# Two layers of gated DeltaNet, short convolution and SwiGLU on one core: other PSUM banks for the side products of two heads, a scaling on another engine, and weight casts in another place

## The chip, the cores and the metric

The kernel runs on one core of one Trainium2 chip. The time is the device time of one execution in microseconds (us); the number that counts is the median of several executions. All arithmetic is in float32. The products of the projections and of the FFN are made of three matmuls each: an operand is cut into a rounded part `hi` and a remainder `lo`, and `hi*hi`, `hi*lo` and `lo*hi` are added in PSUM.

## The reference, cut to what matters

x has 1024 positions of 1024 columns; there are two layers. Each layer is

```
h = rms_norm(x); proj = h @ w_in
q, k, v  = silu(causal conv of 4 taps)            # 4 heads of 128 columns each
o_dn     = gated delta rule of q, k, v, g, beta   # a recurrence over the positions, by chunks
o_sc     = gate_b * conv3(gate_c * hv), normed    # 4 groups of 128 columns
x = x + concat(o_dn normed * silu(z), o_sc) @ w_out
x = x + (silu(rms_norm(x) @ w_gate) * (rms_norm(x) @ w_up)) @ w_down
```

and one last rms_norm follows. The gated delta rule keeps a 128x128 state S per head: S_t = a_t S_{t-1} (I - b_t k_t k_t^T) + b_t v_t k_t^T, o_t = S_t q_t. Each chunk needs the products K K^T and Q K^T of its keys and queries with the decay on them, and keys and values with the positions on the partitions.

## The kernel before, in words

**Halves and chunks.** The 1024 positions are two halves of 512, and a half is four chunks of 128. A tile is mostly 128x512: 128 columns of a head on the partitions and the 512 positions of a half.

**The mixer.** `head(hd, group)` runs the projections of k, q and v for both halves of a head (`kvq`, line 488; 24 matmuls of 128x512 each, two PSUM banks tagged `mm` in turn), each followed by the convolution and the silu on ScalarE (ACT) and VectorE (DVE). The side products of a head are jobs that are put in between the matmuls: after every projection matmul `tick` counts the jobs' lags down, and a job whose lag has run out issues its next piece behind the matmul last issued. They are, for each half:

- `key_tok` (513): four PE transposes of k into one bank, tagged `aux`; ACT copies it out as `kdec` (519) and takes four sums of squares (502).
- `query_tok` (522): four transposes of q into `fx`, and four sums of squares on ACT.
- `gram` (570): K K^T into `aux` (tile `gk`) and Q K^T into `fx` (tile `gq`), each four matmuls of 128x128; DVE multiplies each with the decay into `U` and `A` (584). At its end DVE makes the factor `kd` (587) and scales all of `kdec` with it (588).
- `value_tok` (591): four transposes of v into `aux`, and one DVE operation that reads them (597).

`aux` and `fx` are one bank each (line 75: PS), so that a side product can't be written before the one ahead of it in the same bank has been read. Heads 0 and 1 come first; then `group(0)` inverts and merges (aux) and runs the recurrence `chain` (669) over both, in the banks `ch0`, `ch1` (the steps) and `o0`, `o1` (the outputs). Heads 2 and 3 are projected meanwhile, with their side products in aux and fx. While heads 0 and 1 make their side products, no chain runs: ch0, ch1, o0 and o1 are free, but for the transposes of x's second half at the start of layer 0 (`x_half1`, 319). The short convolution (`sconv`, `sc_norm`) and `gate` use fx and aux too, and `ba` (372) uses fx.

**The FFN's down.** Products are formed by a scheme of seven products P1 to P7 in place of eight (Winograd's form of Strassen's), with the hidden state's operands spilled to HBM and read back (`bprep`, 1145). Twelve blocks (loop of 1210) of seven products handle 18 of the 22 rows of tiles; the last four rows, `tail` (1193), are multiplied plainly at the end (tile `pd`, 1283 to 1288), for each half and each of eight output tiles: four pairs of operand and weight, three matmuls a pair. For these, `tail_half(half)` (1196) loads the hidden operands (`ft`), casts `hi_f` on ACT (897) and subtracts `lo_f` on DVE (898). Half 0's operands are made in the last blocks (1224, 1229); half 1's by `tail_half(1)` at line 1278. Behind it lines 1279 and 1280 load the four weight tiles (`raw_d`, 512 KB each, a ring of three buffers), cast `hi_d` on ACT (195) and subtract `lo_d` on DVE (196). The first `pd` matmuls go into an `mm` bank, which the products P4 and P3 of the last block have just used and which DVE reads at line 1237 (`xT`).

**Order.** Each engine has one queue that it works off strictly in order, the DMA issues among them on SP. The order of every queue is fixed when the kernel is built: a scheduler goes through its own timing of the program and gives each engine, whenever it is free, the instruction that stands first in the program among those that are ready there (operands made, buffer free). So a line's place in the program is its priority, not its place in the queue. `with tc.issue_after(ins)` also puts the instructions that are written in its block and run on the engine of `ins` behind `ins` in that queue, and leaves the other engines' alone.

Of the kernel before, what the change touches and what calls it, by code (L numbers as in the profile page):

```python
# [11 lines left out]
AF = mybir.ActivationFunctionType  # L12
ALU = mybir.AluOpType
# [4 lines left out]
P = 128  # L18
# [33 lines left out]
def tile_hybrid(ctx, tc, x, norm1_g, w_in, dn_conv_w, dn_a_log, dn_dt_bias, dn_norm_g,  # L52
# [3 lines left out]
    V, S, G, PE = nc.vector, nc.scalar, nc.gpsimd, nc.tensor  # L56
# [20 lines left out]
    def sb(tag, name, shape=(P, HALF), dt=F32):  # L77
        if tag == "h":
            return hpool.tile([P, HALF], dt, tag=tag, name=name)
        if tag == "pre":  # L80

            t = prep_.tile([P, 16 + HALF], dt, tag=tag, name=name)
            return t[0:shape[0], 0:shape[-1]] if len(shape) == 2 else t[:, 0:HALF].rearrange("p (c i) -> p c i", i=shape[-1])
        if tag in PB:
            return phase[0].tile(list(shape), dt, tag=tag, bufs=PB[tag], name=name)
        return wp.tile(list(shape), dt, tag=tag, bufs=SB[tag], name=name)
# [5 lines left out]
    def ps_(tag, name, shape=(P, HALF)):  # L92
        return pp.tile(list(shape), F32, tag=tag, bufs=PS[tag], name=name)
# [52 lines left out]
    def full_ap(t):  # L146
        return dram_ap(t, 0, [[128, 128], [USZ, 4], [1, 128]])
# [25 lines left out]
    def split_w(view, name, kd=KD, w=P, eng=None, tags=None):  # L173

        raw = ring.tile([P, kd, w], F32, tag="raw", bufs=3, name=f"raw_{name}")
        dma(raw, view)
        return split_raw(raw, name, eng, tags)
# [12 lines left out]
    def split_raw(raw, name, eng=None, tags=None):  # L190
        if tags:
            hi, lo = [sb(t, f"{p}_{name}", list(raw.shape), F32R) for t, p in zip(tags, ("hi", "lo"))]
        else:
            hi, lo = w_pair(list(raw.shape), name)
        S.copy(hi, raw)
        (eng or V).tensor_tensor(lo, raw, hi.bitcast(F32), ALU.subtract)
        return hi, lo
# [15 lines left out]
    def row_r(ssq, name, stream="n"):  # L213

        m = sm.tile([P, 4], F32, tag="rr", bufs=2, name=f"rr_{name}")
        V.tensor_scalar(m, ssq, 1.0 / D, EPS, ALU.mult, ALU.add)
        y = sm.tile([P, 4], F32, tag="rowr", bufs=4, name=f"rowr_{name}")
        V.tensor_copy(y, rsqrt(m, [P, 4], name, stream))
        return y
# [128 lines left out]
    for l in range(DEPTH):  # L348

        with tc.tile_pool(name=f"mixer{l}", bufs=1, side="right") as phase[0]:  # L350
            w_l = w_in[l]
            hs = [h0, h1]
            sh4 = [P, 4, P]
# [4 lines left out]
            def fx(name, shape=(P, HALF)):  # L358
                return ps_("fx", name, shape)

            def bank(tag):
                return lambda name, shape: ps_(tag, name, shape)

            def wcols(c0, n=P):
                return w_l[:, c0:c0 + n].rearrange("(k p) c -> p k c", p=P)
# [119 lines left out]
            units = {}  # L485
# [12 lines left out]
            def sumsq(ps, dst, nm):  # L498

                sq = sb("sqp", f"sq{nm}", sh4)  # L500
                for c in range(4):
                    S.activation(sq[:, c, :], ps[:, c, :], AF.Square, accum_out=dst[:, c:c + 1])

            def transposed(src, nm, bank):
                t = bank(nm, sh4)
                for c in range(4):
                    PE.transpose(t[:, c, :], src[:, c * P:(c + 1) * P], ident)
                return t
# [4 lines left out]
            def key_tok(hd, half):  # L513

                nm = f"{l}_{hd}_{half}"
                u, ss = units[hd, half], stat(hd)["ss"]
                ktok = transposed(u["k"], f"ktok_{nm}", aux)
                u["kdec"] = sb("kdec", f"kdec_{nm}", sh4)
                S.copy(u["kdec"], ktok)
                sumsq(ktok, ss[:, half * 4:half * 4 + 4], f"k_{nm}")  # L520

            def query_tok(hd, half):
                nm = f"{l}_{hd}_{half}"
                qtok = transposed(units[hd, half]["q"], f"qtok_{nm}", fx)
                sumsq(qtok, stat(hd)["ss"][:, 8 + half * 4:12 + half * 4], f"q_{nm}")

            stats_of = {}
# [1 line left out]
            def stat(hd):  # L529
                if hd not in stats_of:  # L530
                    nm = f"{l}_{hd}"
                    stats_of[hd] = {"ss": s8("ss", nm, 2, 16), "gl": s8("gl", nm, 3)}
                return stats_of[hd]
# [36 lines left out]
            def gram(hd, half, slot):  # L570

                nm = f"{l}_{hd}_{half}"
                u = units[hd, half]
                h4 = slice(half * 4, half * 4 + 4)
                row, c2 = u["row"], u["c2"][:, h4]
                V.tensor_tensor(row, row, c2.unsqueeze(2).broadcast_to(sh4), ALU.mult)
                U = sb("U", f"U_{nm}", sh4)
                A = sb("A", f"A_{nm}", sh4)
                for src, dst in (("k", U), ("q", A)):
                    gp = ps_({"k": "aux", "q": "fx"}[src], f"g{src}_{nm}", sh4)  # L580
                    for c in range(4):
                        cs = slice(c * P, (c + 1) * P)
                        PE.matmul(gp[:, c, :], lhsT=u["k"][:, cs], rhs=u[src][:, cs], start=True, stop=True)
                    V.tensor_tensor(dst, gp, row, ALU.mult)
                dma(full_ap(ud[slot]), U)
                G.tensor_tensor(u["q"], u["q"], u["eta"].rearrange("p c i -> p (c i)"), ALU.mult)
                V.tensor_tensor(u["kd"], u["kd"], c2, ALU.mult)
                V.tensor_tensor(u["kdec"], u["kdec"], u["kd"].unsqueeze(2).broadcast_to(sh4), ALU.mult)
                u.update(U=U, A=A)

            def value_tok(hd, half):
                nm = f"{l}_{hd}_{half}"
                u = units[hd, half]
                h4 = slice(half * 4, half * 4 + 4)
                vtok = transposed(u["v"], f"vtok_{nm}", aux)
                v2 = sb("v2", f"v2_{nm}", sh4)
                V.scalar_tensor_tensor(v2, vtok, 0.5, u["irk"][:, h4].unsqueeze(2).broadcast_to(sh4),
                                       ALU.mult, ALU.mult)
                u["v2"] = v2
# [265 lines left out]
        with tc.tile_pool(name=f"ffn{l}", bufs=1, side="right") as phase[0]:  # L865
# [18 lines left out]
            def stats(acc, name):  # L884
# [3 lines left out]
                        PE.matmul(sp[:, c:c + 1], lhsT=acc[i][:, c * P:(c + 1) * P], rhs=ones1, start=i == 0, stop=i == 1)  # L888
                return row_r(sp[:, 0:4], name)

            def split(src, tags, name, eng=V):
                res = []
                for tag, p in zip(tags, ("hi", "lo")):
                    nm = f"{p}_{name}"
                    res.append(hpool.tile([P, HALF], F32R, tag="h", name=nm) if tag == "h"
                               else sb(tag, nm, (P, HALF), F32R))
                S.copy(res[0], src)  # L897
                eng.tensor_tensor(res[1], src, res[0].bitcast(F32), ALU.subtract)  # L898
                return res

# [124 lines left out]
            for half in range(2):  # L1025
                nm = f"{l}_{half}"
# [22 lines left out]
            for half in range(2):  # L1049
                nm = f"{l}_{half}"  # L1050
# [31 lines left out]
                if half == 0:  # L1082
                    for k in (0, 2, 4, 6, 1, 3, 5, 7):
                        scaled(k)
                        q = "P2" if k % 2 else "P1"
                        B[q].append(split(xh[k], BT[q][k // 2], f"h{q}_{l}_{k}", G))
                else:
# [5 lines left out]
                    def opnd(q, j, src):  # L1093
                        B[q].append(split(src, BT[q][j], f"h{q}_{l}_{j}"))
# [44 lines left out]
            def staged(src, name):  # L1139
                t = sb(STG[stage_n[0] % len(STG)], name)  # L1140
                stage_n[0] += 1
                dma(t, src[:])
                return t

            def bprep(g, q, ops):
                ops[q] = []
                for j in range(GJ):
                    t = staged(hsd[g * GJ + j][q], f"st{q}_{l}_{g}_{j}")
                    ops[q].append(split(t, BT2[q][j], f"d{q}_{l}_{g}_{j}"))
# [43 lines left out]
            tail = list(range(NG * GJ * 2, NF))  # L1193
            hid = {}

            def tail_half(half, part=slice(None)):
                for m in tail[part]:
                    t = staged(hsd[m // 2][("P1", "P2", "P4", "P3")[half * 2 + m % 2]], f"ft{l}_{half}_{m}")
                    hid[half, m] = split(t, (("k", "q"), ("kdec", "v2"))[m % 2] if half else ("h", "h"), f"f{l}_{half}_{m}")
# [10 lines left out]
            for g in range(NG):  # L1210
                for dp in range(4):
                    n = g * 4 + dp
                    nm = f"d{l}_{g}_{dp}"
# [33 lines left out]
            def end(half, acc):  # L1247
# [15 lines left out]
                for c in range(4):  # L1263
# [3 lines left out]
                    for kk in range(2):  # L1267
# [6 lines left out]
                        else:  # L1274
                            V.tensor_scalar(xo, pf, r[:, c:c + 1], None, ALU.mult)
                    dma(out[0, ts_, :], xt)

            tail_half(1)
            wdn = [split_w(ffn_w_down[l][m * P:(m + 1) * P, :].rearrange("p (k c) -> p k c", c=P), f"d{l}_{m}",
                           tags=None if m > tail[0] else ("ub", "yb")) for m in tail]  # L1280
            acc = [[sb("pre", f"acc1_{l}_{h}")] for h in range(2)]
            xg = [[], []]
            for half in range(2):
# [41 lines left out]
```

## Time and profile before

| | us |
|---|---|
| median of 3 runs | 2419.73 |
| lowest, highest run | 2418.4, 2421.8 |
| the profiled execution: its own time | 2423.16 |
| the profiled execution: its span, from first to last instruction | 2421.5 |
| mean granted TensorE clock, as a share of full speed | 0.987 |

The profile is of one execution, which took 3.43 us more than the median; 1.66 us of its time lie outside its span. In its rows a group or an instruction stands as engine, line of the kernel, operation, output<-inputs and shape; a bracket at the end is the idle time of that engine before it and what ended it. A row of the waits gives who waited (engine, tile, line), for what, the total in us, the number of times and the longest. PEclk is the TensorE clock that was granted, as a share of full speed; it has two levels, 1.2 and 2.4 GHz, and a stretch between 0.5 and 1 had some of both. In a timeline, "x4" are four instructions merged.

### The profile page before, as it was taken

The numbers are of one execution on the slowest core, as the hardware profiler recorded it, in microseconds if no ns is written. First come the engines' busy times: TensorE is split into PE (matmuls) and PEld (weight loads), VectorE is DVE, ScalarE is ACT, GpSimd is POOL, SyncE is SP. The second block draws the span as 40 slices with busy tenths as digits, with TensorE's granted clock in tenths as the row PEclk, the third lists the DMA queues.
The fourth block names the chain that finished last, engine by engine and source line by source line (L and its number), as shares of the span: only waits on it lengthen the run. The fifth ranks groups of instructions, "written<-read, shape, count | busy, mean of one in ns | idle before, by whom it ended". The sixth has DMA issues, their size and how long they took to land.

```text
span 2421.5 us, 31888 instructions
## 1 busy us (share of the span) xinstructions
PE 2340.7 (97%) x11522; PEld 1908.2 (79%) x11522; DVE 1622.2 (67%) x2870; ACT 910.3 (38%) x1917; POOL 602.3 (25%) x492
## 2 busy tenths in 40 slices
PE   7999999999999999999998999999999999999998
PEld 5787787887788888788777778878878888887877
DVE  7775773767655655799776666646685565568994
ACT  5524523534323223443344244234342322334334
POOL 3000000031444433234221001000325443422350
PEclk8999999999999999999999999999999999999999
DMA  7222223652333323744322312338423332346531
GB/s 228 66 65 71 65 63 90 204 183 61 109 118 105 113 87 98 248 144 146 106 69 71 76 49 69 77 92 251 124 75 119 106 113 87 109 137 220 160 101 70
DMA packets 362167, 275.21 MB, mean 114 GB/s; under 512 B 47343, under 2 KB 295449, under 8 KB 362009
## 3 DMA queue, kind: packets, MB, share of 16 engines
q1 hardware_dynamic: 362008, 273.18, 37.4%
q8 instruction: 90, 1.47, 0.3%
q14 instruction: 69, 0.56, 0.1%
HBM read 198.08 MB, written 75.04 MB: 113 GB/s over the span
## 4 chain that ended last, share of the span: by engine, by line
PE 73%; DVE 12%; issue 6%; DMA 4%; POOL 3%; ACT 2%; SPq 0%; DVEq 0%; POOLq 0%; ACTq 0%
PE P_g L205 16%; PE P_u L205 14%; PE P_d L205 7%; PE po L205 5%; PE ps_csc L205 4%; PE ps_bsc L205 4%; PE ps_hsc L205 4%; PE pd L205 3%; PE ps_v L205 3%; PE ps_z L205 2%; PE ps_k L205 2%; PE ps_q L205 2%; DMA stP<-hs_P 2%; DMA row<-gd 2%; DVE xT L1237 1%
## 5 line engine op out<-in xcount | busy, mean ns | idle before, releaser
L205 PE MATMUL P_g<-hi_hP,hi_P_g 128*128 128x512 f32 x608 | 239.5, 394 | 3.4 <-DVE u_g L995 1.9
L205 PE MATMUL P_g<-lo_hP,hi_P_g 128*128 128x512 f32 x608 | 238.7, 393 | 3.6 <-DVE lo_hP L898 3.6
L205 PE MATMUL P_u<-hi_hP,hi_P_u 128*128 128x512 f32 x608 | 237.6, 391 | 3.1 <-DVE c_g L1011 2.2
L205 PE MATMUL P_u<-lo_hP,hi_P_u 128*128 128x512 f32 x608 | 237.3, 390 | 0.0
L205 PE MATMUL P_u<-hi_hP,lo_P_u 128*128 128x512 f32 x608 | 237.1, 390 | 0.0
L205 PE MATMUL P_g<-hi_hP,lo_P_g 128*128 128x512 f32 x608 | 236.4, 391 | 0.0
L205 PE MATMUL P_d<-hi_dP,lo_P_d 128*128 128x512 f32 x504 | 196.8, 390 | 3.3 <-DVE lo_P_d L928 3.3
L205 PE MATMUL P_d<-hi_dP,hi_P_d 128*128 128x512 f32 x504 | 196.7, 390 | 2.2 <-ACT hi_dP L897 1.5
L205 PE MATMUL P_d<-lo_dP,hi_P_d 128*128 128x512 f32 x504 | 196.6, 390 | 0.9 <-DVE lo_dP L898 0.9
L205 PEld LDWEIGHTS P_g<-hi_hP,hi_P_g 128*128 128x128 f32 x608 | 114.9, 189 | 30.6 <-DVE u_g L995 2.8
L205 PEld LDWEIGHTS P_g<-lo_hP,hi_P_g 128*128 128x128 f32 x608 | 115.0, 189 | 28.7 <-DVE lo_hP L898 5.2
L205 PEld LDWEIGHTS P_u<-hi_hP,hi_P_u 128*128 128x128 f32 x608 | 114.6, 189 | 28.5 <-DVE c_g L1011 3.1
L205 PEld LDWEIGHTS P_g<-hi_hP,lo_P_g 128*128 128x128 f32 x608 | 114.9, 189 | 23.7
L205 PEld LDWEIGHTS P_u<-lo_hP,hi_P_u 128*128 128x128 f32 x608 | 114.7, 189 | 23.9
L205 PEld LDWEIGHTS P_u<-hi_hP,lo_P_u 128*128 128x128 f32 x608 | 114.4, 188 | 23.7
L1237 DVE TENSOR_TENSOR xT<-P_d,xT 128x512 f32<-128x512 f32 x192 | 125.1, 678 | 3.1 <-PE P_d L205 3.1
L927 ACT CAST hi_P_g<-m_g 128x1024 fp32r<-128x1024 f32 (+1 forms) x64 | 58.8, 919 | 151.9 <-PE P_u L205 127.7
L205 PEld LDWEIGHTS P_d<-hi_dP,lo_P_d 128*128 128x128 f32 x504 | 94.6, 188 | 25.0 <-DVE lo_P_d L928 5.8
L205 PEld LDWEIGHTS P_d<-hi_dP,hi_P_d 128*128 128x128 f32 x504 | 94.6, 188 | 23.6 <-ACT hi_dP L897 2.8
L205 PEld LDWEIGHTS P_d<-lo_dP,hi_P_d 128*128 128x128 f32 x504 | 94.6, 188 | 21.8 <-DVE lo_dP L898 2.2
L898 DVE TENSOR_TENSOR lo_dP<-stP,hi_dP 128x512 fp32r<-128x512 f32 x126 | 96.6, 790 | 18.0 <-ACT hi_dP L897 17.8
L897 ACT CAST hi_dP<-stP 128x512 fp32r<-128x512 f32 x126 | 75.2, 620 | 74.4 <-DMA stP<-hs_P 71.0
(410 smaller groups left out, 5872.0 us busy)
## 6 DMA issues: line engine op xcount, KB each, us to landing
stP<-hs_P SPq DMA_DIRECT2D x126, 256.0 KB, 3.8
m_g<-in_ffn_w_gate_dram SPq DMA_DIRECT2D x46, 512.0 KB, 4.1
m_u<-in_ffn_w_up_dram SPq DMA_DIRECT2D x44, 512.0 KB, 4.4
hs_P<-t SPq DMA_DIRECT2D x72, 256.0 KB, 2.4
m_d<-in_ffn_w_down_dram SPq DMA_DIRECT2D x48, 384.0 KB, 4.1
hs_P<-c_u SPq DMA_DIRECT2D x70, 256.0 KB, 2.0
raw_o<-in_w_out_dram SPq DMA_DIRECT2D x32, 512.0 KB, 4.8
xd<-xT SPq DMA_DIRECT2D x32, 256.0 KB, 2.3
```

The lines of the kernel that those rows point to most:

```text
L205: last_mm[0] = PE.matmul(ps, lhsT=w(k)[i], rhs=m(k)[j], start=k + i + j == 0, stop=k + i == n).ins
L897: S.copy(res[0], src)
L898: eng.tensor_tensor(res[1], src, res[0].bitcast(F32), ALU.subtract)
L927: S.copy(hi, src)
L1237: V.tensor_tensor(t, ps, t, ALU.add)
```

## The change

The side products of heads 0 and 1 (`hd < 2`) go to the recurrence's banks: k's transposes to ch0, q's to ch1, K K^T to o0 and Q K^T to o1. The transposes of v stay in aux for half 0, and go to fx for half 1. Heads 2 and 3 keep aux and fx. For all heads the scaling of kdec becomes four ACT activations of 128x128, one for each chunk, with the factor as a scale per partition. The loads, casts and subtractions of down's last four weights are written ahead of `tail_half(1)`, with their ACT casts behind the last `hi` cast of an operand written before them.

```diff
@@ -358,8 +358,9 @@
             def fx(name, shape=(P, HALF)):
                 return ps_("fx", name, shape)
 
-            def bank(tag):
-                return lambda name, shape: ps_(tag, name, shape)
+            def side(hd, free, tag):
+
+                return lambda name, shape: ps_(free if hd < 2 else tag, name, shape)
 
             def wcols(c0, n=P):
                 return w_l[:, c0:c0 + n].rearrange("(k p) c -> p k c", p=P)
@@ -514,14 +515,14 @@
 
                 nm = f"{l}_{hd}_{half}"
                 u, ss = units[hd, half], stat(hd)["ss"]
-                ktok = transposed(u["k"], f"ktok_{nm}", aux)
+                ktok = transposed(u["k"], f"ktok_{nm}", side(hd, "ch0", "aux"))
                 u["kdec"] = sb("kdec", f"kdec_{nm}", sh4)
                 S.copy(u["kdec"], ktok)
                 sumsq(ktok, ss[:, half * 4:half * 4 + 4], f"k_{nm}")
 
             def query_tok(hd, half):
                 nm = f"{l}_{hd}_{half}"
-                qtok = transposed(units[hd, half]["q"], f"qtok_{nm}", fx)
+                qtok = transposed(units[hd, half]["q"], f"qtok_{nm}", side(hd, "ch1", "fx"))
                 sumsq(qtok, stat(hd)["ss"][:, 8 + half * 4:12 + half * 4], f"q_{nm}")
 
             stats_of = {}
@@ -577,7 +578,7 @@
                 U = sb("U", f"U_{nm}", sh4)
                 A = sb("A", f"A_{nm}", sh4)
                 for src, dst in (("k", U), ("q", A)):
-                    gp = ps_({"k": "aux", "q": "fx"}[src], f"g{src}_{nm}", sh4)
+                    gp = {"k": side(hd, "o0", "aux"), "q": side(hd, "o1", "fx")}[src](f"g{src}_{nm}", sh4)
                     for c in range(4):
                         cs = slice(c * P, (c + 1) * P)
                         PE.matmul(gp[:, c, :], lhsT=u["k"][:, cs], rhs=u[src][:, cs], start=True, stop=True)
@@ -585,14 +586,15 @@
                 dma(full_ap(ud[slot]), U)
                 G.tensor_tensor(u["q"], u["q"], u["eta"].rearrange("p c i -> p (c i)"), ALU.mult)
                 V.tensor_tensor(u["kd"], u["kd"], c2, ALU.mult)
-                V.tensor_tensor(u["kdec"], u["kdec"], u["kd"].unsqueeze(2).broadcast_to(sh4), ALU.mult)
+                for c in range(4):
+                    S.activation(u["kdec"][:, c, :], u["kdec"][:, c, :], AF.Copy, scale=u["kd"][:, c:c + 1])
                 u.update(U=U, A=A)
 
             def value_tok(hd, half):
                 nm = f"{l}_{hd}_{half}"
                 u = units[hd, half]
                 h4 = slice(half * 4, half * 4 + 4)
-                vtok = transposed(u["v"], f"vtok_{nm}", aux)
+                vtok = transposed(u["v"], f"vtok_{nm}", (fx if hd < 2 and half else aux))
                 v2 = sb("v2", f"v2_{nm}", sh4)
                 V.scalar_tensor_tensor(v2, vtok, 0.5, u["irk"][:, h4].unsqueeze(2).broadcast_to(sh4),
                                        ALU.mult, ALU.mult)
@@ -888,13 +890,15 @@
                         PE.matmul(sp[:, c:c + 1], lhsT=acc[i][:, c * P:(c + 1) * P], rhs=ones1, start=i == 0, stop=i == 1)
                 return row_r(sp[:, 0:4], name)
 
+            last_hi = [None]
+
             def split(src, tags, name, eng=V):
                 res = []
                 for tag, p in zip(tags, ("hi", "lo")):
                     nm = f"{p}_{name}"
                     res.append(hpool.tile([P, HALF], F32R, tag="h", name=nm) if tag == "h"
                                else sb(tag, nm, (P, HALF), F32R))
-                S.copy(res[0], src)
+                last_hi[0] = S.copy(res[0], src).ins
                 eng.tensor_tensor(res[1], src, res[0].bitcast(F32), ALU.subtract)
                 return res
 
@@ -1275,9 +1279,10 @@
                             V.tensor_scalar(xo, pf, r[:, c:c + 1], None, ALU.mult)
                     dma(out[0, ts_, :], xt)
 
+            with tc.issue_after(last_hi[0]):
+                wdn = [split_w(ffn_w_down[l][m * P:(m + 1) * P, :].rearrange("p (k c) -> p k c", c=P), f"d{l}_{m}",
+                               tags=None if m > tail[0] else ("ub", "yb")) for m in tail]
             tail_half(1)
-            wdn = [split_w(ffn_w_down[l][m * P:(m + 1) * P, :].rearrange("p (k c) -> p k c", c=P), f"d{l}_{m}",
-                           tags=None if m > tail[0] else ("ub", "yb")) for m in tail]
             acc = [[sb("pre", f"acc1_{l}_{h}")] for h in range(2)]
             xg = [[], []]
             for half in range(2):
```

## Rows read from the trace of the kernel before

**Rows 1.** The page, part 1: busy time and share of the span, by engine.

```profile
PE 2340.7 (97%) x11522; PEld 1908.2 (79%) x11522; DVE 1622.2 (67%) x2870; ACT 910.3 (38%) x1917; POOL 602.3 (25%) x492
```

**Rows 2.** The waits of the PE queue: us in total, times, longest.

```profile
PE ktok L507 <- DVE U L584: 7.5, 2, 3.8
...
PE pd L205 <- DVE lo_d L196: 4.7, 2, 2.3
...
PE pd L205 <- DVE xT L1237: 3.6, 2, 1.8
...
PE vtok L507 <- DVE v L597: 2.3, 3, 1.0
...
PE ot L507 <- ACT sqk L502: 2.1, 2, 1.1
...
PE yp L648 <- ACT R L642: 1.8, 2, 0.9
...
PE vtok L507 <- DVE U L584: 1.5, 1, 1.5
```

**Rows 3.** The timeline of PE, side products of heads 0 and 1: start, us, what.

```profile
100.89 1.11 PE L507 MATMUL ktok<-ident,kT_k 128*128 128x128 f32 x4 [3.84 <-DVE U L584]
...
1286.70 0.66 PE L507 MATMUL ktok<-ident,kT_k 128*128 128x128 f32 x4 [3.70 <-DVE U L584]
...
1288.12 1.07 PE L583 MATMUL gq<-qT_q,kT_k 128*128 128x128 f32 x8
```

**Rows 4.** The timeline of DVE in layer 1, around the U product.

```profile
1282.53 1.28 DVE L588 TENSOR_TENSOR kdec<-kdec,kd 128x512 f32<-128x512 f32 x2
1283.73 1.65 DVE L196 TENSOR_TENSOR lo_z<-raw_z,hi_z 128x1024 fp32r<-128x1024 f32 x1
...
1285.97 0.68 DVE L584 TENSOR_TENSOR U<-gk,row 128x512 f32<-128x512 f32 x1
...
1287.30 0.68 DVE L584 TENSOR_TENSOR A<-gq,row 128x512 f32<-128x512 f32 x1
```

**Rows 5.** Busy time by stretch, PE PEld DVE ACT POOL, PEclk, DMA; stretches of 10 us.

```profile
100.00:110.00 10.00, 9.12 (x46) 7.93 (x47) 7.12 (x16) 5.18 (x18) 1.97 (x3) 0.83 0.56 143
1280.00:1290.00 10.00, 6.30 (x40) 5.15 (x38) 9.84 (x16) 5.95 (x17) 3.04 (x3) 1.00 0.37 92
```

**Rows 6.** Line 588 on DVE: ns min/median/max.

```profile
L588 DVE TENSOR_TENSOR kdec<-kdec,kd x16: 674/684/692, 96.7 to 1497.4; 128x512 f32<-128x512 f32 x16
```

**Rows 7.** The timeline of ACT: four 128x128 activations on SBUF, layer 0.

```profile
84.21 1.26 ACT L567 ACTIVATE row<-row,ngl 128x128 f32<-128x128 f32 x4
```

**Rows 8.** The timeline of PE at the end of down, layer 0.

```profile
1166.12 0.50 PE L205 MATMUL pd<-hi_f,hi_d 128*128 128x512 f32 x1 [1.77 <-DVE xT L1237]
...
1171.24 0.50 PE L205 MATMUL pd<-hi_f,lo_d 128*128 128x512 f32 x1 [2.33 <-DVE lo_d L196]
```

**Rows 9.** The timeline of DVE at the end of down, layer 0.

```profile
1164.80 0.67 DVE L898 TENSOR_TENSOR lo_f<-ft,hi_f 128x512 fp32r<-128x512 f32 x1
1165.40 0.67 DVE L1237 TENSOR_TENSOR xT<-P_d,xT 128x512 f32<-128x512 f32 x1
1166.00 3.46 DVE L898 TENSOR_TENSOR lo_f<-ft,hi_f 128x512 fp32r<-128x512 f32 x3
...
1169.98 1.21 DVE L196 TENSOR_TENSOR lo_d<-raw_d,hi_d 128x1024 fp32r<-128x1024 f32 x1
```

**Rows 10.** The timeline of ACT at the end of down, layer 0.

```profile
1150.62 1.05 ACT L195 CAST hi_d<-raw_d 128x1024 fp32r<-128x1024 f32 x1 [3.51 <-POOL m_d L959]
...
1152.73 0.62 ACT L897 CAST hi_f<-ft 128x512 fp32r<-128x512 f32 x1
...
1162.36 1.05 ACT L195 CAST hi_d<-raw_d 128x1024 fp32r<-128x1024 f32 x1
```

**Rows 11.** The DMA issues of SP at the end of down, layer 0.

```profile
1141.48 14.99 SPq L176 DMA_DIRECT2D raw_d<-in_ffn_w_down_dram  x4
```

**Rows 12.** Busy time by stretch, columns as in rows 5, end of down.

```profile
1170.00:1175.00 5.00, 3.75 (x11) 2.95 (x12) 4.02 (x4) 0.63 (x1) 2.24 (x2) 0.72 0.47 114
```

## The prediction

> **What bounds the kernel now.** I read the page's busy times first: TensorE (PE) is busy for 97% of the span, DVE for 67%, ACT for 38% [rows 1]. So only PE's idle time can be won, plus work that PE does at the lower clock; a cheaper operation elsewhere counts only where PE waits for it. Second come the waits of PE's queue, the list to see what such a change can touch [rows 2]. `ktok` waits 7.5 us, in two places, for the DVE product `U`: a transpose of k that needs the bank aux, in which the K K^T of the other head still lies. `vtok` waits 1.5 us for U and 2.3 us for the `v2` operation of another half: the same bank. The last `pd` products wait 4.7 us for a remainder `lo_d` of the weights and 3.6 us for the add that empties their bank. Third, the timelines at these places.
>
> In PE's timeline the two ktok waits are 3.84 and 3.70 us, one in each layer, at the first k of head 1 [rows 3]. In DVE's timeline U stands behind two kdec scalings (1.28 us together) and a `lo_z` of 1.65 us [rows 4]: bank and DVE together make the stall. After the stall of layer 0 the granted clock is 0.83 over 10 us, so for a third of them it was at the lower of its two levels, 1.2 GHz; after that of layer 1 it stays at 1.00 [rows 5]. At the end of down PE starts `pd` after 1.77 us and stops again, at 1171.24, for 2.33 us [rows 8]. DVE is working without a pause there: it makes the four `lo_f` of half 1 (0.67 us and 3.46 us), needed only eight output tiles later, ahead of the last lo_d [rows 9]. Its cast, hi_d, was there at 1163.4 [rows 10], so lo_d at 1169.98 was late by its place in the queue alone. The clock is 0.72 in the 5 us that follow [rows 12]. Layer 1 repeats this end of down.
>
> **The change, part by part.** *Banks of k and q.* No instruction is added or taken away. ktok in ch0 no longer waits for U: in layer 1 it could start at 1286.70 - 3.70 = 1283.00. What is late next is the gram of the half behind it, which now needs o0 and o1 instead of aux and fx. It comes 1.42 us after ktok [rows 3], at 1284.42, and there U and A of the half before must have been read: at 1286.65 and 1287.98, or 1.28 us sooner without the scalings, 1285.37 and 1286.70 [rows 4]. If K K^T goes first, it waits 0.95 us and Q K^T some 0.4 us behind it; if Q K^T goes first (as in rows 3), 2.3 us. I take 1.9 us left over. Saved: 3.84 + 3.70 - 2 x 1.9 = 3.7 us; bounds 2.8 (Q K^T first in both) and 7.5 (DVE's queue gets U and A earlier too). For the clock of layer 0, 10 us at 0.83 cost 1.7 us; a stall of about half the length may or may not bring it, as the two layers show, so I take half, 0.85 us; bounds 0 and 1.7.
>
> *Banks of v.* Half 0 in aux no longer meets U, half 1 in fx no longer meets half 0's v2. PE's waits of 2.3 + 1.5 = 3.8 us [rows 2] go whole; bound below 1.9, if data arrive as late in half of them.
>
> *The scaling on ACT.* Gone from DVE are 16 operations (4 heads, 2 halves, 2 layers) of 0.684 us [rows 6], 10.9 us; what that is worth is in the 1.28 us above, and elsewhere I count nothing, since DVE is busy two thirds of the time. Added on ACT are 64 activations of 128x128 on SBUF with an operand per partition. Before shows none of just this form; the nearest are the exponentials of the same shape on SBUF, four in 1.26 us [rows 7]; so 16 x 1.26 = 20.2 us of ACT. ACT is 38% busy and kdec is read only by the chain, so most is covered by ACT's idle time. Where it isn't, a burst stands ahead of an ACT operation that PE waits for: PE does so for `ot` and for `yp` in four places [rows 2]. One burst ahead of each would cost 4 x 1.26 = 5.0 us; a gain of up to 2 us is the other end, as DVE's makers of k, q and v come sooner. I take one burst paid, +1.3 us. The Trainium skill ("ScalarE: Activation LUTs", Rules for kernel authors) says to put multiplications on VectorE rather than ScalarE; rows 6 and 7 do show the four ACT instructions taking almost twice DVE's one, but they load the less busy engine.
>
> *Down's last weights.* Four loads on SP, four casts on ACT and four subtractions on DVE are written earlier, ahead of half 1's operands. On DVE the last lo_d then precedes up to four lo_f. SP is passed by the half-1 operands' loads only on paper: the weights' loads go from 1141.48 to 1156.5, when a ring buffer comes free [rows 11], and those of `ft` need other buffers. On ACT the first hi_d, now at 1150.62, must go behind the hi_f at 1152.73 [rows 10], so it moves by some 2.7 us; the two casts and that hi_f move up by 1.05 us. Its lo_d is first needed at 1166, so 12 us cover that; without the cover it would be 2.7 us. What each lo_d frees for the next load is delayed as much, but two of the loads wait on other subtractions, which move up. So the 2.33 us go in each layer: 4.7 us [rows 2]. The other wait, for the add that empties the mm bank (1165.40, rows 9), I leave as it is: with lo_d (1.21 us) ahead of it instead of one lo_f (0.67 us) it grows by 0.5 us, with neither it shrinks by 0.7; with both layers, +1.1 to -1.3 us. The lower clock costs 5 x (1 - 0.72) = 1.4 us a layer; one short stall instead of two may avoid it: half, 1.4 us in all; bounds 0 and 2.8.
>
> **The sum.** -3.7 - 0.85 - 3.8 + 1.3 - 4.7 - 1.4 = -13.2 us. The profiled execution took 2423.16 us, so the same execution would take 2410.0; it stands 3.43 us above the median of the runs shown, so the median to forecast is 2406.6. With all ends good: -7.5 - 1.7 - 3.8 - 2 - 4.7 - 1.3 - 2.8 = -23.8, 2395.9; with all bad: -2.8 - 1.9 + 5.0 - 4.7 + 1.1 = -3.3, 2416.4.
>
> **The rivals.** *The wait only moves (17%).* DVE, not the bank, is what is late: U and A come after the same lo_z and convolution steps, and PE, 3.7 us sooner, stops at the gram, or at a next k that isn't made yet. For it: DVE is 98% busy in the 10 us before the stall of layer 1 [rows 5]. Against it: the projections of q, v and z that follow need no side product. Then the mixers give half of v's 3.8 us, less the burst, and down its 6.1: -1.9 + 1.3 - 6.1 = -6.7 us, 2413.0.
>
> *The order in down does not turn (12%).* If in the scheduler's timing the last weight lands late, half 1's operands still go first, and the 6.1 us stay. Then 2406.6 + 6.1 = 2412.7. For it: hi_d came behind three of half 1's hi_f on ACT already [rows 10]. Against it: priority now speaks for lo_d, and its cast was ready 6.5 us before.
>
> *Nothing to speak of (15%).* The order of the queues is fixed in the scheduler's timing, which is not the chip's; moved banks shuffle every queue of the mixer, and new waits of 1 to 4 us as in rows 2 eat what the old ones gave: about 2419.7, between 2415 and 2424.
>
> *ACT becomes the late engine, slower (12%).* Each of the 16 bursts stands in ACT's queue, and behind it the copies that empty the mm banks, and in heads 2 and 3 the copies `vn` between two steps of the chain. If every burst is paid in full, +20.2 us stand against the gains without the burst, 14.5: +5.7, 2425.4. It decides from twelve bursts of sixteen on (12 x 1.26 = 15.1). For it: PE already waits for ACT in the merges (`yp`, rows 2). Against it: ACT has idle time in every stretch of 10 us in rows 5 (half of it), and the burst can lie there. The rule that the Trainium skill states in "ScalarE: Activation LUTs" (above) would make it this case, 2425.4.
>
> **How the numbers follow.** The forecast's own case has 44%, from 2396 to 2416. With it the first two rivals, both below 2414.9, make "faster" 0.44 + 0.17 + 0.12 = 0.73, of which I give 0.02 to "no change", because both lie within 2 us of the bound; a measurement of this kernel can tell 0.2%, 4.8 us, from no change. So faster 0.71, same 0.17, slower 0.12. The range of 8 in 10 starts at 2396 and takes in the first half of "nothing to speak of", to 2421; outside are the slower case and the rest of that one, some 0.19.
>
> **What would show it.** In the changed profile: no PE wait of ktok for U and none of vtok for v2 or U at heads 0 and 1, gk or gq waiting some 2 us for U or A instead; no line 588 on DVE, and 64 ACT activations, four in some 1.26 us; no wait of pd for lo_d, with the last lo_d ahead of lo_f on DVE; the clock at 1.00 behind `pd`'s start. It would be wrong if PE's waits on ACT in the mixers grew by more than 5 us, if the gram's waits took the whole 7.5 us, or if lo_d stood behind lo_f still.

## The result, and the profile after

The changed kernel takes 2397.51 us (median of 4 runs, 2394.61 to 2400.03), the kernel before 2420.76 in the same comparison: ratio 0.9905, 95% interval 0.9888 to 0.9922. A later comparison gave 2397.46 us and 0.9909 (0.9897 to 0.9922). So the change saves 21 to 23 us; 13.2 were forecast, and the time lies inside the range, 1.5 us above its lower end. The execution profiled first took 2395.95 us, with a span of 2394.2 and a mean granted clock of 0.991; before, the span was 2421.5 and the clock 0.987.

The busy times, to be read against [rows 1]:

```profile
PE 2330.9 (97%) x11522; PEld 1902.4 (79%) x11522; DVE 1615.2 (67%) x2854; ACT 928.0 (39%) x1981; POOL 601.7 (25%) x492
```

PE has as many instructions as before; DVE has 16 fewer, ACT 64 more. The waits of PE's queue in the changed kernel (us in total, times, longest), to be read against [rows 2]:

```profile
PE pd L205 <- DVE xT L1241: 3.0, 2, 1.5
...
PE bc_n L224 <- DVE rowr_n L218: 2.1, 1, 2.1
...
PE ot L508 <- ACT sqk L503: 2.0, 2, 1.0
...
PE xtp L328 <- DMA xp<-in_x_dram: 1.9, 1, 1.9
...
PE yp L650 <- ACT R L644: 1.8, 2, 0.9
...
PE pd L205 <- DVE lo_d L196: 0.9, 2, 0.5
```

The 7.5 us of `ktok` for `U` and the 3.8 us of `vtok` are gone, `pd`'s 4.7 us for `lo_d` are 0.9, and the waits on ACT in the mixers have not grown. PE's timeline at the first k of head 1 in each layer, with the gram behind it, shows how (start, us, what; idle time before it in brackets, none here); compare [rows 3]:

```profile
95.30 0.60 PE L508 MATMUL ktok<-ident,kT_k 128*128 128x128 f32 x4
96.66 1.05 PE L584 MATMUL gk<-kT_k 128*128 128x128 f32 x8
...
1267.57 0.60 PE L508 MATMUL ktok<-ident,kT_k 128*128 128x128 f32 x4
1268.94 1.05 PE L584 MATMUL gk<-kT_k 128*128 128x128 f32 x8
```

No `gk` waits, though the forecast left 1.9 us there in each layer. DVE's timeline says why; compare [rows 4]:

```profile
92.54 0.23 DVE L588 TENSOR_TENSOR kd<-kd,c 128x4 f32<-128x4 f32 x2
92.68 1.22 DVE L196 TENSOR_TENSOR lo_z<-raw_z,hi_z 128x1024 fp32r<-128x1024 f32 x1
93.82 1.79 DVE L481 SCALAR_TENSOR_TENSOR y_k<-pre_k,cst,y_k 128x512 f32<-128x512 f32 x1
95.53 0.68 DVE L585 TENSOR_TENSOR U<-gk,row 128x512 f32<-128x512 f32 x1
...
1267.75 0.68 DVE L585 TENSOR_TENSOR U<-gk,row 128x512 f32<-128x512 f32 x1
...
1270.34 1.21 DVE L196 TENSOR_TENSOR lo_z<-raw_z,hi_z 128x1024 fp32r<-128x1024 f32 x1
```

U has read its bank at 96.21 and 1268.43, before `gk` wants it at 96.66 and 1268.94. In layer 1 `lo_z` now stands behind U; in layer 0 it still stands ahead.

The end of down in layer 0: PE, then DVE; compare [rows 8, 9].

```profile
1153.71 0.47 PE L205 MATMUL pd<-hi_f,hi_d 128*128 128x512 f32 x1 [1.42 <-DVE xT L1241]
...
1156.93 0.50 PE L205 MATMUL pd<-hi_f,lo_d 128*128 128x512 f32 x1 [0.47 <-DVE lo_d L196]
```

```profile
1152.29 0.67 DVE L902 TENSOR_TENSOR lo_f<-ft,hi_f 128x512 fp32r<-128x512 f32 x1
1152.89 0.68 DVE L1241 TENSOR_TENSOR xT<-P_d,xT 128x512 f32<-128x512 f32 x1
1153.49 1.16 DVE L902 TENSOR_TENSOR lo_f<-ft,hi_f 128x512 fp32r<-128x512 f32 x1
1154.57 2.31 DVE L196 TENSOR_TENSOR lo_d<-raw_d,hi_d 128x1024 fp32r<-128x1024 f32 x1
...
1157.40 2.38 DVE L902 TENSOR_TENSOR lo_f<-ft,hi_f 128x512 fp32r<-128x512 f32 x2
```

The last `lo_d` is ahead of two of the four `lo_f`, not of all, and the add that empties the mm bank has one ahead of it. That is the 1.42 and the 0.47 us left. The windows (PE, PEld, DVE, ACT, POOL busy, granted clock, DMA); compare [rows 5, 12]:

```profile
100.00:110.00 10.00, 10.00 (x52) 8.36 (x51) 6.71 (x15) 7.15 (x26) 0.92 (x3) 1.00 0.31 74
196.00:211.00 15.00, 13.07 (x142) 9.78 (x142) 5.51 (x14) 4.39 (x13) 0.00 (x0) 1.00 0.32 82
...
1155.00:1160.00 5.00, 4.44 (x19) 3.11 (x18) 5.00 (x5) 0.00 (x0) 2.57 (x3) 1.00 0.38 100
```

The clock behind both stalls is 1.00, where it was 0.83 and 0.72. The span times one minus the mean clock estimates what the lower level took: 2421.5 x 0.013 = 31.5 us before, 2394.2 x 0.009 = 21.5 after (1.2 us either way, for the third decimal of the clock). PE's busy time, for the same number of instructions, is 9.8 us less, which agrees. Of the 27.3 us between the two spans about 10 are clock and 17 are PE's waits.

These two executions lie 4 us further apart than the medians, so the split is better taken from all runs on record. On average over 40 runs of the kernel before the clock is 0.9870 and the lower level takes 31.4 us; over the eight of the changed kernel it is 0.9909 and 21.9. So of some 23 us 9.5 are clock, give or take one, and 13 to 14 are waits; the forecast had 2.25 and 10.9.

### The profile page after: what moved, and what is told of

It reads as the page before. It is cut to its first block, busy times and chain, and to the rows that moved or that the text cites. A ratio compares the mean times of both kernels' runs of the same rounds, so it can differ in the third digit from the quotient of the medians.

```text
span 2394.2 us, 31939 instructions
## 1 busy us (share of the span) xinstructions
PE 2330.9 (97%) x11522; PEld 1902.4 (79%) x11522; DVE 1615.2 (67%) x2854; ACT 928.0 (39%) x1981; POOL 601.7 (25%) x492
## 4 chain that ended last, share of the span: by engine, by line
PE 78%; DVE 10%; issue 6%; POOL 2%; DMA 2%; ACT 2%; SPq 0%; DVEq 0%; POOLq 0%; ACTq 0%
PE P_g L205 16%; PE P_u L205 14%; PE P_d L205 8%; PE po L205 5%; PE ps_csc L205 4%; PE ps_bsc L205 4%; PE ps_hsc L205 4%; PE pd L205 3%; PE ps_v L205 3%; PE ps_z L205 3%; PE ps_k L205 3%; PE ps_q L205 3%; DVE xT L1241 1%; DVE lo_hP L902 1%; DVE lo_P_d L932 1%
```

## The experiments

Each run has its ratio to the kernel before in the same comparison, with the 95% interval; 0.0010 is 2.4 us. The first three make one part of the change alone in the kernel before.

**Banks alone.** `kdec` stays on DVE, down's order stays the old one:

```diff
-ktok = transposed(u["k"], f"ktok_{nm}", aux)
+ktok = transposed(u["k"], f"ktok_{nm}", side(hd, "ch0", "aux"))
...
-vtok = transposed(u["v"], f"vtok_{nm}", aux)
+vtok = transposed(u["v"], f"vtok_{nm}", (fx if hd < 2 and half else aux))
```

> The kernel before with the bank moves of the change alone (k, q, their products and the values of heads 0 and 1); kdec stays on VectorE, the order at the end of down stays the old one. Theory 'banks': the mixers' gain of about 14.5 us and the start's 1.6 us are the banks' own; about 2420.8 - 16.1 = 2404.7 us, no gram wait over 0.5 us in PE's queue. Theory 'VectorE': the moved banks alone leave the forecast's rest, because U and A still stand behind two kdec and a lo_z; gk or gq wait some 1.9 us in each layer, about 2410 us.

Measured: 2408.9 us against 2420.93, ratio 0.995 (0.9935 to 0.9965), so 12.1 us saved; the mean clock is 0.990. PE's timeline in layer 0 (first and second gram), then in layer 1:

```profile
93.37 1.05 PE L584 MATMUL gk<-kT_k 128*128 128x128 f32 x8
...
99.60 1.16 PE L584 MATMUL gk<-kT_k 128*128 128x128 f32 x8 [1.08 <-DVE U L585]
100.93 1.16 PE L584 MATMUL gq<-qT_q,kT_k 128*128 128x128 f32 x8 [0.17 <-DVE A L585]
...
1272.24 1.05 PE L584 MATMUL gk<-kT_k 128*128 128x128 f32 x8
...
1277.22 1.05 PE L584 MATMUL gk<-kT_k 128*128 128x128 f32 x8
```

Neither theory had it whole: the gram does wait, 1.25 us, in layer 0 only. DVE's timeline of the same kernel shows `ss`, the start of the chain of small operations that makes the head's norms, and U:

```profile
88.06 0.17 DVE L540 TENSOR_SCALAR ss<-ss 128x16 f32<-128x16 f32 x1
...
98.87 0.68 DVE L585 TENSOR_TENSOR U<-gk,row 128x512 f32<-128x512 f32 x1
...
1265.53 0.17 DVE L540 TENSOR_SCALAR ss<-ss 128x16 f32<-128x16 f32 x1
...
1276.03 0.68 DVE L585 TENSOR_TENSOR U<-gk,row 128x512 f32<-128x512 f32 x1
```

In the kernel before the same rows are, on PE and on DVE:

```profile
93.27 1.05 PE L583 MATMUL gk<-kT_k 128*128 128x128 f32 x8
...
1279.22 1.05 PE L583 MATMUL gk<-kT_k 128*128 128x128 f32 x8
```

```profile
89.34 0.17 DVE L539 TENSOR_SCALAR ss<-ss 128x16 f32<-128x16 f32 x1
...
100.15 0.68 DVE L584 TENSOR_TENSOR U<-gk,row 128x512 f32<-128x512 f32 x1
...
1275.75 0.20 DVE L539 TENSOR_SCALAR ss<-ss 128x16 f32<-128x16 f32 x1
```

`ss` comes 5.31 and 6.71 us ahead of the first `gk`, where it came 3.93 and 3.47 ahead: 1.38 and 3.24 us sooner. U comes 5.50 and 3.79 us behind that `gk`, where it came 6.88 (at 100.15) and 6.75 (at 1285.97, [rows 4]) behind: 1.38 and 2.96 us sooner. So the banks also move DVE's queue forward. That this is because `ss` needs the sums of squares of k and q, whose transposes no longer wait for a bank, is argued from the code and was not tried apart.

**Scaling alone**, in the kernel before:

```diff
-V.tensor_tensor(u["kdec"], u["kdec"], u["kd"].unsqueeze(2).broadcast_to(sh4), ALU.mult)
+for c in range(4):
+    S.activation(u["kdec"][:, c, :], u["kdec"][:, c, :], AF.Copy, scale=u["kd"][:, c:c + 1])
```

> The kernel before with the kdec scaling on ScalarE alone. Theory 'banks': ktok still waits for the bank of the gram, nothing moves by more than 1 us: 2420.8 us, within 2. Theory 'VectorE': U and A come 1.3 to 3 us sooner in each layer, so the two ktok stalls of 3.84 and 3.70 us shrink by that much: 2415 to 2418 us. A third, that ScalarE is now late for ot and yp: slower, up to 2425 us.

Measured: 2414.64 us, ratio 0.9977 (0.9967 to 0.9987): 5.6 us saved, clock 0.989. That is just past the better end of the theory 'VectorE', 2415. Its PE waits:

```profile
PE ktok L507 <- DVE U L584: 4.0, 2, 2.0
...
PE vtok L507 <- DVE v L598: 1.6, 4, 0.6
...
PE vtok L507 <- DVE U L584: 0.6, 1, 0.6
```

`ktok` waits 3.5 us less than in [rows 2], `vtok` 1.6 us less. PE's and DVE's timelines in layer 0:

```profile
99.16 0.66 PE L507 MATMUL ktok<-ident,kT_k 128*128 128x128 f32 x4 [2.04 <-DVE U L584]
```

```profile
96.63 1.21 DVE L196 TENSOR_TENSOR lo_z<-raw_z,hi_z 128x1024 fp32r<-128x1024 f32 x1
...
98.43 0.68 DVE L584 TENSOR_TENSOR U<-gk,row 128x512 f32<-128x512 f32 x1
```

U comes at 98.43 instead of 100.15, 1.7 us sooner: the two `kdec` of 1.28 us are no longer ahead of it, and `lo_z` took 1.21 us instead of 1.65. `ktok`'s stall is 1.8 us shorter, all of it. So the trace shows what the theory says; what it is worth in time is less clear, as the table below shows.

**Down's weights alone**, in the kernel before:

```diff
-S.copy(res[0], src)
+last_hi[0] = S.copy(res[0], src).ins
...
+with tc.issue_after(last_hi[0]):
+    wdn = [split_w(...) for m in tail]
 tail_half(1)
-wdn = [split_w(...) for m in tail]
```

> The kernel before with the moved weights of down alone. Theory 'order': the last lo_d stands earlier on VectorE and the two pd waits for it (2.33 us a layer) and the lower clock behind them go: 6.9 us, about 2413.9 us. Rival 'part': only the lower clock goes or only the waits, 2416 to 2418 us. Rival 'the mixers did it': the tail gives nothing by itself, 2420.8 us.

Measured: 2415.24 us, ratio 0.9972 (0.9961 to 0.9983): 6.8 us by the ratio, 5.7 by the medians. `pd` waits 0.9 us for lo_d and 2.9 for the add, 4.5 us less than in [rows 2]. The theory 'order' holds. The three parts sum to 12.1 + 5.6 + 6.8 = 24.5 us; all together gave 23.0 by the ratio of the first comparison: they add up, within the intervals.

The clock of every run is on record, so what the lower level took on average can be set beside each saving. The standard errors of these averages are 0.5 to 1.8 us.

| | runs | mean clock | lower level, us | less than before, us |
|---|---|---|---|---|
| before, beside the three parts | 18 | 0.9867 | 32.1 | |
| banks alone | 6 | 0.9892 | 26.1 | 6.0 |
| scaling alone | 12 | 0.9893 | 25.7 | 6.4 |
| down's weights alone | 7 | 0.9879 | 29.3 | 2.8 |

So about half of what the banks and the weights save is clock. For the scaling alone the clock is as large as the whole saving. In its one profile PE's idle time is 5.1 us less than in the profile before, but what is left of the span without the lower level's share is on average 2387.9 us, and 2387.2 before. How much of the 5.6 us is wait stays open, and whether shorter stalls are what raised the clock was not tried apart.

The next four take one part back out of the changed kernel, or alter it. **Scaling back on VectorE:**

```diff
-for c in range(4):
-    S.activation(u["kdec"][:, c, :], ..., AF.Copy, scale=u["kd"][:, c:c + 1])
+V.tensor_tensor(u["kdec"], u["kdec"], u["kd"].unsqueeze(2).broadcast_to(sh4), ALU.mult)
```

> The changed kernel with the kdec scaling back on VectorE. Theory 'banks': U and A come early enough without the move to ScalarE; 2397.5 to 2399 us. Theory 'VectorE': the gram waits for U and A again, 1.3 to 1.9 us in each layer, and a lower clock may follow in layer 0: 2401 to 2403 us.

Measured: 2404.9 us, ratio 0.9926 (0.9914 to 0.9937); the changed kernel's is 0.9905 or 0.9909. That is 4 to 5 us by the ratios (7.4 by the medians), at the edge of what the intervals tell apart, and of the size of the scaling alone. `gk` waits 1.3 us for U and `gq` 0.2 for A, in one layer; the rest is not in a wait of this place. The mean clock of its five runs is 0.9890, so the lower level takes 26.4 us, 4.5 more than in the changed kernel. The theory 'VectorE' fits best, as far as the waits in one layer go.

**Values back in aux:**

```diff
-vtok = transposed(u["v"], f"vtok_{nm}", (fx if hd < 2 and half else aux))
+vtok = transposed(u["v"], f"vtok_{nm}", aux)
```

> The changed kernel with the values of half 1 of heads 0 and 1 back in the bank aux. Theory 'the bank made vtok wait': the wait of vtok for v2 comes back, since half 1's transposes want the bank that half 0's v2 still reads; 1.9 us a layer at most, 2399 to 2401 us. Theory 'data': with k gone from aux and VectorE earlier, v2 has been done by the time half 1 needs the bank; 2397.5 us, within 1.

Measured: 2407.44 us, ratio 0.9947 (0.9934 to 0.996), 9 to 10 us slower than the changed kernel and clear of its interval: more than the first theory's most. `vtok` waits 4.9 us in all for `v2`; its PE timeline in layers 0 and 1 has the two longest:

```profile
106.88 0.66 PE L508 MATMUL vtok<-ident,vT_v 128*128 128x128 f32 x4 [1.88 <-DVE v L599]
...
1284.57 0.66 PE L508 MATMUL vtok<-ident,vT_v 128*128 128x128 f32 x4 [2.30 <-DVE v L599]
```

The wait for half 0's `v2` is larger than in [rows 2], where 2.3 us stood: PE asks for the bank while v2 still has to read it, and v2 comes later, 4.01 us behind half 0's transposes in layer 1 where it came 2.64 us behind them before. The mean clock of the six runs is 0.9890, so the lower level takes 26.5 us, 4.6 more than in the changed kernel. Wait and clock together are the 9 to 10 us.

**No hold on the moved weights:**

```diff
-with tc.issue_after(last_hi[0]):
-    wdn = [split_w(...) for m in tail]
+wdn = [split_w(...) for m in tail]
 tail_half(1)
```

> The changed kernel with down's last weights written ahead of half 1's operands, but not held behind the last cast of half 0. Theory 'the hold matters': the first hi_d goes ahead of casts of half 0's operands on ScalarE again and these come late for pd's first groups; 1 to 3 us slower, 2398.5 to 2400.5 us. Theory 'the place in the program is enough': 2397.5 us, within 1.

Measured: 2400.44 us, ratio 0.9917 (0.9904 to 0.9931). `pd` waits 3.8 us for the add (3.0 with the hold) and 0.5 for lo_d (0.9). The 2 to 3 us are in the sense of 'the hold matters', but the intervals overlap: not settled.

**The first k back in aux**, against the start of the program:

```diff
-ktok = transposed(u["k"], f"ktok_{nm}", side(hd, "ch0", "aux"))
+ktok = transposed(u["k"], f"ktok_{nm}", aux if (l, hd, half) == (0, 0, 0) else side(hd, "ch0", "aux"))
```

> The changed kernel with the very first k of the program (layer 0, head 0, half 0) back in the bank aux, so that ch0 is not taken at the start. Theory 'start': the transposes of x go back to their old place at the head of PE's queue and the 5.8 us wait for the transfer of x comes back; net 1.6 us slower, about 2399 us. Theory 'noise': the start's difference is none of the bank's, 2397.5 us, within 0.5.

Measured: 2397.08 us, ratio 0.9905 (0.989 to 0.992), no change. PE's wait for the transfer of x is 5.7 us again, where the changed kernel had 1.9 and the kernel before 5.8, and the time stays:

```profile
PE xtp L328 <- DMA xp<-in_x_dram: 5.7, 1, 5.7
```

The theory 'start' falls: what the changed kernel gains there it gives back, most of it soon. The first gram starts at 92.25 us here and at 91.68 in the changed kernel, so 0.6 of 3.8 us are left. A wait of `bc_n` of 2.1 us, which this run does not have, is part of that.

**The end of down, three ways.** First other banks for `pd`, then half 1's subtractions behind the last lo_d, then both; with the changed kernel itself beside the last two:

```diff
-ps = ps_(("mm", "mm", "aux", "ch0", "ch1", "o0", "o1")[cnt[2] % 7], f"pd{l}_{d}_{half}")
+ps = ps_(("aux", "ch0", "ch1", "o0", "o1", "mm", "mm")[cnt[2] % 7], f"pd{l}_{d}_{half}")
```

> The changed kernel with the banks of the last pd groups taken in another order: the five that are free first, the two mm banks, which the last adds of up still read, last. Theory 'bank': the wait of pd of 1.42 us and 1.6 us for that add goes in both layers; about 2394.5 us. Theory 'data': pd then waits at the same place for a lo_f or lo_d that comes no sooner, 2397.5 us, within 1.

```diff
-        (eng or V).tensor_tensor(lo, raw, hi.bitcast(F32), ALU.subtract)
+        last_lo[0] = (eng or V).tensor_tensor(lo, raw, hi.bitcast(F32), ALU.subtract).ins
...
-tail_half(1)
+with tc.issue_after(last_lo[0]):
+    tail_half(1)
```

> The changed kernel with the subtractions of half 1's operands held behind the last lo_d on VectorE. Theory 'order': two lo_f (0.6 and 1.16 us) still stand ahead of the add that empties the mm bank and of the last lo_d; behind it they cost nothing, since half 1 is needed eight output tiles later. pd's waits of 3.0 and 0.9 us shrink by 2 us in all, about 2395.5 us. Theory 'data': VectorE then waits for hi_d or raw_d instead, 2397.5 us, within 1.

> The same, with the free banks taken first by pd as in e7. Theory 'order': the lo_d wait of 2.2 us a layer that e7 put in the place of the bank's goes with the two lo_f, so that nearly all of pd's 3.9 us and the lower clock behind it go: about 2394 us. Theory 'VectorE bounds the end of down': lo_d is late by VectorE's own work whatever stands ahead, pd waits 1 to 2 us a layer for it, 2397 to 2400 us.

> The changed kernel once more, unaltered, for a median and a profile on the same chip as the three kernels beside it. If the low-clock stretch at 201 to 208 us, which e1, e4, e5, e6, e7 and e8 show and the first profile of the changed kernel does not, is no property of the change, it shows up here; the median is 2397.5 us, within 2.

Measured: banks alone 2401.78 us, ratio 0.9918 (0.9904 to 0.9931); late half alone 2397.4 us, 0.9915 (0.99 to 0.9929); both 2395.64 us, 0.9892 (0.9877 to 0.9907); the changed kernel beside them 0.9909. With the banks alone the wait only changes its name, as its second theory said (its time, 2397.5, was missed by 4 us).

```profile
1160.67 0.50 PE L205 MATMUL pd<-hi_f,lo_d 128*128 128x512 f32 x1 [2.05 <-DVE lo_d L196]
```

The adds that empty the mm banks are those of down, line 1241, not of up as the expectation has it. With the late half alone the wait for lo_d is gone and `pd` waits 3.6 us, four times, for adds, so the 2 us of its theory 'order' did not come. With both, the windows of the end of down in layers 0 and 1:

```profile
1155.00:1165.00 10.00, 10.00 (x45) 7.96 (x44) 10.00 (x11) 3.15 (x4) 5.19 (x3) 1.00 0.58 159
2328.00:2340.00 12.00, 12.00 (x53) 9.66 (x52) 10.78 (x12) 3.09 (x6) 5.19 (x3) 1.00 0.00 0
```

PE does not stop at all there. Two waits, one for a bank and one for a weight, lay one behind the other, and only taking both away shows in PE's idle time. In the time, 1.8 us less by the medians, it can't be told from the changed kernel; the mean clock of its five runs is lower, 0.9898 against 0.9909, which takes back 2.5 us of what the waits gave. It is the lowest median of all, so it is kept as the best version with that reserve.

The changed kernel's second profile has a span of 2395.6 and a clock of 0.992; its window at the first merge shows what the expectation asked, columns as above:

```profile
196.00:211.00 15.00, 13.02 (x133) 9.89 (x132) 5.06 (x13) 3.79 (x10) 0.00 (x0) 0.77 0.29 75
```

Here the same kernel had 1.00 in one execution and 0.77 in the other, with PE idle for the same 2 us. So the clock in a single stretch is no property of the change; only the average over many runs tells something of it.

**No scaling at all.** The scaling of `kdec` by `kd` is left out on every engine:

```diff
-for c in range(4):
-    S.activation(u["kdec"][:, c, :], u["kdec"][:, c, :], AF.Copy, scale=u["kd"][:, c:c + 1])
```

> The changed kernel without the kdec scaling on any engine (the scaling of kdec by kd is left out). Theory 'covered': the 64 activations lie in ScalarE's idle time and cost nothing, 2397.5 us, within 1.5. Theory 'burst paid', the forecast's term: some 1.3 us faster, and up to 5 us if a burst stands ahead of each ScalarE operation that PE waits for: 2392.5 to 2396 us.

Measured: 2398.24 us, ratio 0.9918 (0.9906 to 0.9929), beside 0.9909 (0.9897 to 0.9922) with the scaling: not faster. The intervals exclude the 5 us of the second theory, but not its 1.3. The changed kernel's groups of instructions have the price, 20.6 us for all 64, so 1.29 a burst of four, since neighbours overlap:

```profile
L590 ACT ACTIVATE kdec<-kdec,kd 128x128 f32<-128x128 f32 x64 | 20.6, 391 | 7.6 <-DVE kd L588 7.3
```

PE's waits say whether a burst was paid where the forecast looked for it: `ot` and `yp` wait 2.0 and 1.8 us with the scaling on ACT and 2.0 and 1.8 without any. Theory 'covered' holds at these places.

## Why the prediction was right in its sign and short in its size

The direction, the places and three of the mechanisms were right; the sum fell short by 10 us. The term that was most mis-sized is the clock, 2.25 us forecast and 9.5 measured; the waits came to 13 or 14 us instead of 10.9. That the time still lies in the range is partly luck: the clock went past its good end (1.7 + 2.8 = 4.5 us), and the waits stayed well short of their good end (19.3 us). Step by step:

- **The clock** (-0.85 and -1.4 us): 9.5 on average over all runs. The stretches that were named, behind `ktok` in layer 0 and behind `pd`'s start, did go to 1.00. What failed is that the forecast counted the lower level only there. It took 31.4 us before, spread over other stretches too, in the merges and at the start of gate and up among them, and these change from one execution to the next. Why they became fewer on average stays open; no run takes the clock apart from the waits.
- **Banks of k and q** (-3.7 us, and -0.85 for the clock) and **of v** (-3.8): together 8.35 us, 12.1 measured for the banks alone. The step that failed is "I take 1.9 us left over". It held U's and A's times of [rows 4] fixed while moving PE. In the runs DVE's queue moved too: U came 1.4 and 3.0 us sooner after the first gram by the banks alone, and 1.25 us of gram wait were left in all instead of 3.8, none in the whole change. The good bound of 7.5 us named this ("DVE's queue gets U and A earlier too"). In the total it shows less: 6 of the 12.1 us are clock.
- **The scaling on ACT** (+1.3 us): the term of the wrong sign. It is -5.6 us alone and -4 to -5 inside the change, by the ratios; how much of it is wait and how much clock stays open. "One burst paid" is not seen in PE's waits for `ot` and `yp`, which did not grow; the run without any scaling can't tell 1.3 us from none. The length of a burst was right: 1.29 us, 1.26 forecast. What was missed is on DVE: "elsewhere I count nothing, since DVE is busy two thirds of the time". DVE's share is an average; around U it had no pause, and with U 1.7 us sooner PE's stall was 1.8 us shorter in layer 0.
- **Down's last weights** (-4.7 and -1.4 us): 5.7 to 6.8 measured, right, with 2.8 of it clock. The wait for lo_d is 0.9 instead of none, since two lo_f still go first, and the add's wait shrank by 0.6 us [rows 2], inside the stated -1.3 to +1.1.

Two slips in the working change nothing: the lower bound of 2.8 us for the banks of k and q comes out as 2.9 (7.54 - 2 x 2.3), and the 98% of DVE [rows 5] belong to the stretch that holds the stall, not to the one before it.

Of the rivals, "the wait only moves" fell with `gk`'s missing wait, "the order in down does not turn" with the 0.9 us, "nothing to speak of" with the interval, and "ACT becomes the late engine" with 2.0 and 1.8 us of waits for `ot` and `yp`, as before. The rule that the Trainium skill states in "ScalarE: Activation LUTs" (Rules for kernel authors), multiplications on VectorE, would have made it that case. The trace agrees on the price (1.29 us for a burst, 0.684 on DVE [rows 6]) and not on the outcome: here the dearer way, on the engine that PE did not wait for at this place, is the faster one.

## What to carry to other kernels

When a bank move lets one engine run ahead, redo the times of the engine that feeds it as well: what it makes for others may move by as much as the wait itself. Price work by the pauses around the critical instruction, not by the busy share of the span: 1.28 us of scaling ahead of a product that PE waits for went into PE's stall whole, and the same work on an engine with pauses added nothing to the waits looked at. Put the lower clock of the whole program into the sum, not of two stretches, and take it from several runs: here it was 9.5 of 23 us. If two waits follow each other within a few us, take both away before judging either.

## What was not expected of the hardware

A DVE instruction beside one on POOL can take as long as POOL's. In the kernel before, the two small `kd` products ran beside POOL's multiply of q, shown here on DVE and on POOL:

```profile
95.42 1.33 DVE L587 TENSOR_TENSOR kd<-kd,c 128x4 f32<-128x4 f32 x2
```

```profile
95.31 1.34 POOL L586 TENSOR_TENSOR qT_q<-qT_q,eta 128x512 f32<-128x512 f32 x1 [3.78 <-PE gq L583]
```

They end at 96.75, POOL's at 96.65. In the changed kernel they took 0.23 us, ahead of POOL's multiply, and then it was `y_k` at 93.82 that took 1.79 us, beside it; the next two y_k, at 96.13 and 97.57, took 0.84 and 0.73. At the end of down `lo_d`, begun while POOL added, took 2.31 us; before, begun 0.16 us ahead of POOL's add, it took 1.21 [rows 9], and the add took 2.20 where two others took 1.68 each. POOL's timeline at `y_k`:

```profile
93.72 1.34 POOL L587 TENSOR_TENSOR qT_q<-qT_q,eta 128x512 f32<-128x512 f32 x1 [5.54 <-PE gq L584]
```

So the 1.1 us won at `kd` in layer 0 were lost again two instructions on. The Trainium skill ("SBUF — State Buffer", section "SBUF: two separate sides") says that VectorE with two operands in SBUF and GpSimd share a pair of ports under an exclusive lock, and the loser blocks for the whole instruction. These rows agree with it, in both directions; no run here moved POOL's work to test it.
